# Hybrid MLA/GLA block: finer second norm, eight modulation columns computed later

## Chip, cores and metric

One core of one Trainium2 chip runs the whole kernel. The metric is device time of one execution in microseconds. It is the median of three runs.

## What is computed

One decoder block in float32 for 512 tokens of width 2048. Two token mixers (latent attention and gated linear attention) run side by side, and a SwiGLU feed-forward network follows. Both halves are normed before and after, and modulated by six vectors that are linear in silu(c). The part that the change touches is this:

```python
ada = silu(c) @ w_ada + b_ada                       # 6 x 2048 columns
shift_m, scale_m, gate_m, shift_f, scale_f, gate_f = split(ada, 6)
...
o = concat([o_mla, o_gla]) @ w_out
x = x + gate_m * rms_norm(o, g_post_mix)            # first half of the second norm
h = rms_norm(x, g_pre_ffn) * (1 + scale_f) + shift_f
f = (silu(h @ w_gate) * (h @ w_up)) @ w_down
x = x + gate_f * rms_norm(f, g_post_ffn)
```

## The kernel before

**Products.** Each float32 weight block of 128 x 2048 is loaded by SP into one of four buffers of the pool `wr` and split into a rounded part and a remainder. ACT makes the first (`CAST`, L202 and L910), DVE the second (`TENSOR_TENSOR`, L203 and L911). Both land in eight buffers `wh`. Three matmuls (L214 to L216) make one product.

**Modulation columns.** `ada` (L224) loads 1 MB of `w_ada` into a `wr` buffer (L227), and one DVE operation (L228) multiplies it by the broadcast silu(c) and sums each row: 128 of the 12288 columns. The broadcast itself holds one `wr` buffer until the last of them. The generator `ada_rest` hands out 64 of these steps, one for each `next(more)`: gate_m, scale_f, shift_f, gate_f, in blocks of 16. The filler steps consume them: `fill_qk` four per step, `fill_vr` three, `fill_out` one or two.

**Output projection.** `out_group` (L881) multiplies the GLA half of the mixed rows by a column block n of `w_out`, in two steps q. It adds the attention half that was spilled earlier (L891), sums squares (L892) and multiplies by gate and gain (L893). Column block 0 is done for all four token tiles. Then blocks 1 to 3 are done for tiles 0 and 1 (th = 0), and for tiles 2 and 3 (th = 1).

**Second norm.** `second_norm(t)` takes one token tile: row scale, residual add (L808), squares (L810), second row scale. Then for each n it scales the rows (L817), transposes four 128 x 128 pieces on PE (L820) and modulates them on ACT (L826). The columns land in `h2`. It is a generator, and `advance(k)` takes k steps of it. The norms of tiles 0 and 1 are advanced in the projection of th = 1. Those of tiles 2 and 3 are advanced in the early products.

**Early products and forms.** The feed-forward network uses a seven-product scheme on a 2 x 2 split (token half by feature half). Each of its inputs is a form, a block of `h2` or a sum of blocks, split into two parts by `parts` (ACT `CAST` L837, DVE L838). The differences are DVE `minus` (L842). The first six blocks (`PRO` = 6) compute two of the products early, 12 banks of 48 matmuls, from the forms a11 and a12. These need tiles 0 and 1 alone. Meanwhile `more_forms` makes s1, s3, s2, a22 and s4, which need tiles 2 and 3. The main loop uses these from its first products on. A finished bank is emptied by ACT (L940) or DVE (`vadd`, L928).

**Order.** A scheduler places the instructions on each engine's queue from the order of the program and from pool releases. Each queue runs in order.

Of the kernel before, what the change touches and what calls it, by code (L numbers as in the profile page):

```python
# [14 lines left out]
AF = mybir.ActivationFunctionType  # L15
ALU = mybir.AluOpType
# [4 lines left out]
P = 128  # L21
S = 512
D = 2048
KT = D // P
DFF = 5632
NT = S // P
# [51 lines left out]
def block_kernel(ctx, tc, x, c, pos, w_ada, cols, w_g1, w_kqvr, w_uq, w_uk, w_uv, wg17,  # L78
# [9 lines left out]
    V, A, T = nc.vector, nc.scalar, nc.tensor  # L88
# [22 lines left out]
    def t2(dt=F32, n=512):  # L111
        return sp.tile([P, n], dt, tag="t2k", name=nm("t"))

    def bank(g):
        return pp.tile([P, 512], F32, tag="ps" + g, name=nm("ps"), bufs=4)
# [18 lines left out]
    bias = cp.tile([P, 4], F32, name="bias")  # L134
# [3 lines left out]
    ident = cs[:, K_ID:K_ID + P]  # L138
# [6 lines left out]
    for n in range(4):  # L145
        ps = bank("A")
# [4 lines left out]
    def rsqrt(src, n, w=1):  # L151

        v, y, b = small(w, "rv"), small(w, "ry"), small(w, "rb")
        V.tensor_scalar(v, src, 1.0 / n, EPS, op0=ALU.mult, op1=ALU.add)
        last_act[0] = A.activation(y, v, AF.Sqrt)
        V.reciprocal(y, y)
        V.scalar_tensor_tensor(out=b, in0=v, scalar=-0.5, in1=y, op0=ALU.mult, op1=ALU.mult)
        V.tensor_tensor(out=b, in0=b, in1=y, op=ALU.mult)
        V.scalar_tensor_tensor(out=y, in0=b, scalar=1.5, in1=y, op0=ALU.add, op1=ALU.mult)
        return y  # L160
# [30 lines left out]
    def load_split(src, nkt, ncol):  # L191

        raw = wp.tile([P, 2048], F32, tag="wr", name=nm("wr"))
        dma(out=raw[:, :nkt * ncol], in_=src)
        per = 1024 // ncol if ncol <= 1024 else 1
        parts = []
        for k0 in range(0, nkt, per):
            n = min(per, nkt - k0) * ncol
            r = raw[:, k0 * ncol:k0 * ncol + n]
            hi = wp.tile([P, 1024], F32R, tag="wh", name=nm("hi"), bufs=8)  # L200
            lo = wp.tile([P, 1024], F32R, tag="wh", name=nm("lo"), bufs=8)
            A.copy(out=hi[:, :n], in_=r)  # L202
            V.tensor_tensor(out=lo[:, :n], in0=r, in1=hi[:, :n], op=ALU.subtract)  # L203
            for k in range(min(per, nkt - k0)):
                parts.append((hi[:, k * ncol:(k + 1) * ncol], lo[:, k * ncol:(k + 1) * ncol]))
        return parts
# [27 lines left out]
    scol = cp.tile([P, 32], F32, name="scol")  # L234
    shcol = cp.tile([P, 32], F32, name="shcol")
# [33 lines left out]
    for t in range(NT):  # L269
        for n in range(4):  # L270
            acc, xx = xs[:, 4 * t + n:4 * t + n + 1], xt_[t][n]
            if t == NT - 1:
                V.tensor_tensor_reduce(out=sq[1], in0=xx, in1=xx, scale=1.0, scalar=0.0,
                                       op0=ALU.mult, op1=ALU.add, accum_out=acc)
# [140 lines left out]
    for which, src in ((0, ang), (1, al)):  # L415
        ps = bank("B")
# [39 lines left out]
    def fill_qk():  # L456
        for half in range(2):
            pss = [bank("A") for _ in range(4)]
            for kq in (2, 3):
                w = load_split(w_kqvr[half, kq], 4, 512)  # L460
                for _ in range(4):
                    next(more)
                for k, b in ORDER[kq == 3]:
                    mm3(pss[b], cut(w[k], b * P, P), hT[4 * kq + k], kq + k == 2, kq + k == 6)
                if kq == 3:
                    add_up(pss, qk[4 * half:4 * half + 4])
                    qk[4 * half:4 * half + 4] = spill(qk[4 * half:4 * half + 4], "qk")
                yield
# [327 lines left out]
    x1d = [dp.tile([P, D], F32, name=f"x1d{t}") for t in range(NT)]  # L796
    mixg = [split_new(o) for o in mixg]
    osum = cp.tile([P, 16], F32, name="osum")
    def second_norm(t):
        v = small(1, "v1")  # L800
        V.tensor_reduce(out=v, in_=osum[:, 4 * t:4 * t + 4], axis=AX.X, op=ALU.add)
        v = rsqrt(v, D)
        xs = small(4, "xs")
        xt = wp.tile([P, 2048], F32, tag="wr", name=nm("wr"))
        dma(out=xt, in_=x[t])
        for n in range(4):
            xs_ = xt[:, n * 512:(n + 1) * 512]
            V.scalar_tensor_tensor(out=og[t][n], in0=og[t][n], scalar=v, in1=xs_, op0=ALU.mult, op1=ALU.add)  # L808
            dma2(out=x1d[t][:, n * 512:(n + 1) * 512], in_=og[t][n])
            A.activation(xs_, og[t][n], AF.Square, accum_out=xs[:, n:n + 1])  # L810
        v2 = small(1, "v2")
        V.tensor_reduce(out=v2, in_=xs, axis=AX.X, op=ALU.add)
        v2 = rsqrt(v2, D)
        yield
        for n in range(4):
            y = t2()
            A.activation(y, og[t][n], AF.Copy, scale=v2)  # L817
            ps = bank("B")
            for k in range(4):
                T.transpose(ps[:, k * P:(k + 1) * P], y[:, k * P:(k + 1) * P], ident)  # L820
            for k in range(4):
                kk = 4 * n + k
                if kk % 2 == 0 and t % 2 == 0:
                    h2[t // 2][kk // 2] = t2()
                o = (kk % 2) * 256 + (t % 2) * P
                A.activation(h2[t // 2][kk // 2][:, o:o + P], ps[:, k * P:(k + 1) * P], AF.Identity,  # L826
                             scale=scol[:, 16 + kk:17 + kk], bias=shcol[:, 16 + kk:17 + kk])
            yield

# [3 lines left out]
    def parts(src):  # L835
        hi, lo = t2(F32R), t2(F32R)
        A.copy(out=hi, in_=src)  # L837
        V.tensor_tensor(out=lo, in0=src, in1=hi, op=ALU.subtract)  # L838
        return hi, lo

    def minus(out, a, b):
        V.tensor_tensor(out=out, in0=a, in1=b, op=ALU.subtract)  # L842
# [1 line left out]
    h2 = [[None] * 8, [None] * 8]  # L844
    form = {n: [None] * 4 for n in ("a11", "a12", "a22", "s1", "s2", "s3", "s4")}

    def first_forms():
        for j in range(4):
            form["a11"][j] = parts(h2[0][j])
            yield  # L850
        for j in range(4):
            form["a12"][j] = parts(h2[0][4 + j])
            yield

    def more_forms():
        s2 = [None] * 4
        for j in range(4):
            a11, a21, a22 = h2[0][j], h2[1][j], h2[1][4 + j]
            s1 = t2()
            minus(s1, a21, a22)  # L860
            form["s1"][j] = parts(s1)
            minus(a21, a21, a11)
            form["s3"][j] = parts(a21)
            minus(a11, a11, s1)
            s2[j] = a11
            form["s2"][j] = parts(a11)
            yield
        for j in range(4):
            form["a22"][j] = parts(h2[1][4 + j])
            a12 = h2[0][4 + j]  # L870
            minus(a12, a12, s2[j])
            form["s4"][j] = parts(a12)
            yield

    norms = iter(())

    def advance(n):
        for _ in range(n):
            next(norms, None)

    def out_group(n, toks, steps=0):  # L881
        pss = {t: bank("A") for t in toks}
        for q in range(2):
            w = load_split(w_out[n, 2 + q], 4, 512)
            for k in range(4):
                for t in toks:
                    mm3(pss[t], cut(mixg[4 * q + k], t * P, P), w[k], q + k == 0, q + k == 4)
            advance(steps)
        for t in toks:
            o = og[t][n] = fetch(og[t][n])  # L890
            V.tensor_tensor(out=o, in0=pss[t], in1=o, op=ALU.add)  # L891
            A.activation(pss[t], o, AF.Square, accum_out=osum[:, 4 * t + n:4 * t + n + 1])  # L892
            V.tensor_tensor(out=o, in0=o, in1=ggm[n], op=ALU.mult)  # L893
# [3 lines left out]
    for th in range(2):  # L897
        toks = (2 * th, 2 * th + 1)
        for n in range(1, 4):
            out_group(n, toks, 3)  # L900
        advance(30)
        norms = itertools.chain(*[second_norm(t) for t in toks], (first_forms, more_forms)[th]())


    def wtile():
# [2 lines left out]
    def wparts(src):  # L908
        hi, lo = wtile(), wtile()
        A.copy(out=hi, in_=src)  # L910
        V.tensor_tensor(out=lo, in0=src, in1=hi, op=ALU.subtract)  # L911
        return hi, lo
# [6 lines left out]
    def up_product(ps, w, f, s, first, last):  # L919

        for kk in range(4):
            rh = cut(form[f][2 * s + kk // 2], (kk % 2) * 256, 256)
            for b in range(2):
                mm3(ps[:, b * 256:(b + 1) * 256], cut(w, kk * 256 + b * P, P), rh,
                    first and kk + b == 0, last and kk + b == 4)
# [5 lines left out]
    for j in range(PRO):  # L931
        raws = [raw_of(w_fg[j, s]) for s in range(2)]
        q1, sg = t2(), t2()
        for f, o in (("a11", 0), ("a12", 1024)):
            ps = bank("A")
            for s in range(2):
                up_product(ps, wparts(raws[s][:, o:o + 1024]), f, s, s == 0, s == 1)
                advance(2)
            if f == "a11":
                A.copy(out=q1, in_=ps)  # L940
        vadd(sg, ps, q1)
        A.activation(sg, sg, AF.Silu)
        early.append((q1, sg))
    advance(30)

    gd = []
    gate_f = gate_out(1)
# [230 lines left out]
```

## Time and profile before

| | |
|---|---|
| median of three runs | 2164.9 us (2156.6 to 2166.36) |
| profiled execution, its own time | 2170.64 us |
| its span | 2168.9 us |
| PE busy | 2081.8 us (96%) |
| DVE busy | 1752.8 us (81%) |
| ACT busy | 918.8 us (42%) |

Times on the timeline count from the start of the span. The granted TensorE clock is a share of full speed. A busy PE can still be at half clock, so idle time and clock are read together, stage by stage.

### The profile page before, as it was taken

To read this page: it belongs to the slowest core of one execution; us is meant where nothing else is said; L and a number is where in the kernel's file an instruction comes from. 1 tells how busy PE (TensorE), PEld (TensorE's weight loads), DVE (VectorE), ACT (ScalarE), POOL (GpSimd) and SP (SyncE) were. 2 spreads that over 40 slices of the span, in tenths; PEclk is the share of its full clock that TensorE was granted. 3 is DMA by queue.
4 is the path that set the end of the run, shared out by engine and by line. 5 is a ranking of instruction groups with operands and counts; after the bars stand their busy time and mean duration, and the time that the engine had idled before them with its cause. 6 is when DMAs were issued, how large, how long until landed. Compare 5 with 4: busy or idle time off the path is not lost.

```text
span 2168.9 us, 31978 instructions
## 1 busy us (share of the span) xinstructions
PE 2081.8 (96%) x12714; PEld 1841.0 (85%) x12714; DVE 1752.8 (81%) x2236; ACT 918.8 (42%) x1277; POOL 206.0 (9%) x387
## 2 busy tenths in 40 slices
PE   7999999999899996999999999999999999999998
PEld 5888767776688875999999999999999988888876
DVE  6888987667466676789998898888888877988998
ACT  5433223233332487444344444444444454333342
POOL 0000000001111010010011011011001031221000
PEclk9999999999899997999999999999999999999999
DMA  8886787567365564354544344343344665564534
GB/s 335 303 323 235 278 304 270 221 229 269 119 244 212 185 244 172 120 197 165 205 160 166 127 165 156 127 175 147 127 175 150 274 261 205 213 237 155 206 116 156
DMA packets 85818, 440.56 MB, mean 203 GB/s; under 512 B 12297, under 2 KB 12409, under 8 KB 48034
## 3 DMA queue, kind: packets, MB, share of 16 engines
q1 hardware_dynamic: 55440, 340.16, 42.8%
q0 software_dynamic: 30224, 98.33, 12.0%
q8 instruction: 100, 1.64, 0.3%
q14 instruction: 52, 0.42, 0.1%
q10 hardware_dynamic: 2, 0.01, 0.0%
HBM read 379.19 MB, written 59.26 MB: 202 GB/s over the span
## 4 chain that ended last, share of the span: by engine, by line
PE 70%; issue 15%; DVE 8%; DMA 5%; ACT 1%; POOL 1%; SPq 0%; DVEq 0%; ACTq 0%; POOLq 0%
PE ps L214 22%; PE ps L215 22%; PE ps L216 22%; DMA wr<-w_ada 3%; DVE wr L228 2%; DVE t L928 1%; DMA wr<-w_kqvr 1%; DVE wh L911 1%; DVE lo L203 1%; PE ps L584 1%; PE ps L611 1%; DVE wr L928 1%; PE ps L583 1%; DMA t<-x 0%; DMA wr<-w_uq 0%
## 5 line engine op out<-in xcount | busy, mean ns | idle before, releaser
L214 PE MATMUL ps<-t,wh 128*128 128x256 f32 x2464 | 703.0, 285 | 20.9 <-DVE t L928 8.2
L910 ACT CAST wh<-wr 128x1024 fp32r<-128x1024 f32 x448 | 464.7, 1051 | 592.8 <-PE ps L215 335.1
L216 PE MATMUL ps<-t,wh 128*128 128x256 f32 x2464 | 701.1, 285 | 2.9 <-DVE wh L911 2.7
L215 PE MATMUL ps<-t,wh 128*128 128x256 f32 x2464 | 701.5, 285 | 0.0
L911 DVE TENSOR_TENSOR wh<-wr,wh 128x1024 fp32r<-128x1024 f32 x448 | 540.7, 1220 | 141.1 <-ACT wh L910 138.2
L214 PEld LDWEIGHTS ps<-t,wh 128*128 128x128 f32 x2464 | 477.5, 194 | 23.4 <-issue 8.4
L216 PEld LDWEIGHTS ps<-t,wh 128*128 128x128 f32 x2464 | 477.0, 194 | 3.5 <-DVE wh L911 3.5
L215 PEld LDWEIGHTS ps<-t,wh 128*128 128x128 f32 x2464 | 477.5, 194 | 0.0
L228 DVE CUSTOM_DVE_ANT_0 wr<-wr,cB 128x2048 f32<-128x2048 f32 x96 | 219.3, 2286 | 47.7 <-DMA wr<-w_ada 47.4
L202 ACT CAST hi<-wr 128x1024 fp32r<-128x1024 f32 (+3 forms) x122 | 122.6, 1009 | 241.8 <-PE ps L215 145.2
L215 PE MATMUL ps<-wh,t 128*128 128x512 f32 x560 | 218.1, 389 | 3.0 <-DVE wh L911 3.0
L216 PE MATMUL ps<-wh,t 128*128 128x512 f32 x560 | 217.7, 389 | 0.0
L214 PE MATMUL ps<-wh,t 128*128 128x512 f32 x560 | 217.2, 389 | 0.0
L928 DVE TENSOR_TENSOR wr<-wr,wr 128x1024 f32<-128x1024 f32 (+1 forms) x128 | 198.7, 1554 | 16.2 <-DMA wr<-w_fd 13.9
L203 DVE TENSOR_TENSOR lo<-wr,hi 128x1024 fp32r<-128x1024 f32 (+3 forms) x122 | 141.9, 1168 | 55.9 <-ACT hi L202 53.9
L214 PE MATMUL ps<-t,hi 128*128 128x512 f32 x432 | 169.5, 400 | 5.2 <-DVE t L313 2.4
L215 PE MATMUL ps<-t,hi 128*128 128x512 f32 x432 | 171.3, 397 | 2.5 <-DVE t L306 2.4
L216 PE MATMUL ps<-t,lo 128*128 128x512 f32 x432 | 169.6, 394 | 0.0
L214 PE MATMUL ps<-hi,t 128*128 128x512 f32 x400 | 161.6, 404 | 1.2 <-DVE t L209 0.9
L928 DVE TENSOR_TENSOR t<-ps,t 128x512 f32<-128x512 f32 x222 | 149.6, 683 | 9.4 <-issue 7.9
L215 PE MATMUL ps<-lo,t 128*128 128x512 f32 x400 | 156.8, 392 | 0.0
L216 PE MATMUL ps<-hi,t 128*128 128x512 f32 x400 | 156.2, 393 | 0.0
(229 smaller groups left out, 2427.9 us busy)
## 6 DMA issues: line engine op xcount, KB each, us to landing
wr<-w_ada SPq DMA_DIRECT2D x96, 1024.0 KB, 5.6
wr<-w_fg SPq DMA_DIRECT2D x56, 1024.0 KB, 4.9
wr<-w_fu SPq DMA_DIRECT2D x44, 1024.0 KB, 7.1
wr<-w_fd SPq DMA_DIRECT2D x40, 1024.0 KB, 5.9
gd<-t POOLq DMA_DIRECT2D x148, 256.0 KB, 2.7
t<-gd POOLq DMA_DIRECT2D x112, 256.0 KB, 4.6
wr<-w_kqvr SPq DMA_DIRECT2D x24, 1024.0 KB, 5.0
wr<-w_out SPq DMA_DIRECT2D x22, 1024.0 KB, 5.8
```

The lines of the kernel that those rows point to most:

```text
L202: A.copy(out=hi[:, :n], in_=r)
L203: V.tensor_tensor(out=lo[:, :n], in0=r, in1=hi[:, :n], op=ALU.subtract)
L214: T.matmul(ps, lhsT=a, rhs=c_, start=start, stop=False)
L215: T.matmul(ps, lhsT=a, rhs=d_, start=False, stop=False)
L216: T.matmul(ps, lhsT=b, rhs=c_, start=False, stop=stop)
L228: V.tensor_tensor_reduce(out=raw, in0=raw, in1=cB, scale=1.0, scalar=0.0, op0=ALU.mult, op1=ALU.add, accum_out=adac[:, j:j + 1])
L583: T.matmul(sc[:, :W], lhsT=qn[hh][:, qs], rhs=kn[hh][:, :W], start=True, stop=False)
L584: T.matmul(sc[:, :W], lhsT=qr[rows, qs], rhs=krope[rows, :W], start=False, stop=True)
L611: T.matmul(po[:, qs], lhsT=vh[j][:, (h % 4) * P:(h % 4 + 1) * P], rhs=pT[:, j * P:(j + 1) * P], start=(j == 0), stop=(j == i))
L910: A.copy(out=hi, in_=src)
L911: V.tensor_tensor(out=lo, in0=src, in1=hi, op=ALU.subtract)
L928: V.tensor_tensor(out=out, in0=a, in1=b, op=ALU.add)
```

## The change

`fill_qk` takes two modulation steps instead of four, in four steps of the program: eight fewer there. The later fillers take the same numbers as before, and `out_group` now takes one after each load of `w_out`. The 64 steps are used up within th = 0.

The second norm takes a pair of tiles. Both residuals come first. The rows of column block i + 1 are scaled while block i is turned (transposed and modulated). After each block of both tiles the forms that it completes are made, one per step. For tiles 2 and 3 the blocks go in the order 0, 2, 1, 3. The fourth of each four modulations goes to DVE as a `tensor_scalar`. The 30 forced steps between the halves are gone, and the chain of norms goes on. In the early products two steps are taken per product for the first two blocks and one after that. A loop takes more steps where a form is missing.

```diff
             for kq in (2, 3):
                 w = load_split(w_kqvr[half, kq], 4, 512)
-                for _ in range(4):
+                for _ in range(2):
                     next(more)
...
-    def second_norm(t):
+    def residual(t):
...
-        v2 = rsqrt(v2, D)
+        return rsqrt(v2, D)
+
+    def scaled(t, n, v2):
+        ys[t][n] = y = t2()
+        A.activation(y, og[t][n], AF.Copy, scale=v2)
+
+    def turned(t, n):
+
+        ps = bank("B")
+        for k in range(4):
+            T.transpose(ps[:, k * P:(k + 1) * P], ys[t][n][:, k * P:(k + 1) * P], ident)
...
+            if k == 3:
+                V.tensor_scalar(dst, src, sc, sh, op0=ALU.mult, op1=ALU.add)
+            else:
+                A.activation(dst, src, AF.Identity, scale=sc, bias=sh)
+
+    def second_norm(toks, order, then):
+
+        a, b = toks
+        va = residual(a)
         yield
...
+        vb = residual(b)
+        yield
+        for i, n in enumerate(order):
+            if i == 0:
+                scaled(a, n, va)
+                scaled(b, n, vb)
+                yield
+            if i < 3:
+                scaled(a, order[i + 1], va)
+            turned(a, n)
             yield
+            if i < 3:
+                scaled(b, order[i + 1], vb)
+            turned(b, n)
+            yield
+            for _ in then(i):
+                yield
...
+    def more_forms(i):
+        if i % 2 == 0:
+            return
+        for j in (i - 1, i):
...
             form["s1"][j] = parts(s1)
+            yield
             minus(a21, a21, a11)
             form["s3"][j] = parts(a21)
+            yield
...
             w = load_split(w_out[n, 2 + q], 4, 512)
+            next(more)
...
-        advance(30)
-        norms = itertools.chain(*[second_norm(t) for t in toks], (first_forms, more_forms)[th]())
+        norms = itertools.chain(norms, second_norm(toks, ORDERS[th], (first_forms, more_forms)[th]))
+    while form["a11"][1] is None:
+        advance(1)
...
-                up_product(ps, wparts(raws[s][:, o:o + 1024]), f, s, s == 0, s == 1)
-                advance(2)
+                w = wparts(raws[s][:, o:o + 1024])
+                while form[f][2 * s + 1] is None:
+                    advance(1)
+                up_product(ps, w, f, s, s == 0, s == 1)
+                advance(2 if j < 2 else 1)
```

On the SP queue, the loads of the output projection stood like this before (`wr` is the weight pool, L194 a weight load, L805 the load of x for a residual):

```order
L194 DMA wr_5508<-w_out 128x2048
L194 DMA wr_5542<-w_out 128x2048
L194 DMA wr_5588<-w_out 128x2048
L805 DMA wr_5634<-x 128x2048
L194 DMA wr_5685<-w_out 128x2048
L805 DMA wr_5757<-x 128x2048
L194 DMA wr_5794<-w_out 128x2048
```

and stand like this now (L808 is the load of x):

```order
L194 DMA wr_5502<-w_out 128x2048
L227 DMA wr_5512<-w_ada 128x2048
L194 DMA wr_5539<-w_out 128x2048
L227 DMA wr_5549<-w_ada 128x2048
L194 DMA wr_5588<-w_out 128x2048
L808 DMA wr_5634<-x 128x2048
L808 DMA wr_5671<-x 128x2048
L194 DMA wr_5700<-w_out 128x2048
```

The modulation loads alternate with the weight loads, and the second load of x moved ahead of the second weight load of th = 1.

On the DVE queue, column blocks 2 and 3 of th = 0 stood like this before (L203 is a remainder of `w_out`, L891 and L893 empty the banks of a block):

```order
L203 TENSOR_TENSOR lo_5511<-wr_5508,hi_5510 128x1024
L203 TENSOR_TENSOR lo_5515<-wr_5508,hi_5514 128x1024
L203 TENSOR_TENSOR lo_5545<-wr_5542,hi_5544 128x1024
L891 TENSOR_TENSOR t_5496<-ps_5426,t_5496 128x512
L891 TENSOR_TENSOR t_5501<-ps_5427,t_5501 128x512
L203 TENSOR_TENSOR lo_5549<-wr_5542,hi_5548 128x1024
```

and stand like this now (L923 empties the banks, L228 is the modulation step):

```order
L203 TENSOR_TENSOR lo_5505<-wr_5502,hi_5504 128x1024
L228 ISA wr_5512,adac<-wr_5512,cB 128x2048
L203 TENSOR_TENSOR lo_5509<-wr_5502,hi_5508 128x1024
L923 TENSOR_TENSOR t_5490<-ps_5414,t_5490 128x512
L923 TENSOR_TENSOR t_5495<-ps_5415,t_5495 128x512
L203 TENSOR_TENSOR lo_5542<-wr_5539,hi_5541 128x1024
```

One modulation step now stands among the four remainders of each column block, ahead of the two that empty the banks.

On the ACT queue, the norms of tiles 2 and 3 in the early products stood like this before (L817 scales rows, L826 modulates, L810 sums squares, L940 empties a bank):

```order
L817 ACTIVATE t_6100<-t_5336,ry_6092 128x512
L910 CAST wh_6579<-wr_6528 128x1024
L826 ACTIVATE t_6107<-ps_6102,shcol,scol 128x128 x2
L826 ACTIVATE t_6110<-ps_6102,shcol,scol 128x128 x2
L817 ACTIVATE t_6141<-t_5782,ry_6092 128x512
L810 ACTIVATE wr_6222,xs_6221<-t_5341 128x512
L810 ACTIVATE wr_6222,xs_6221<-t_5787 128x512
L826 ACTIVATE t_6148<-ps_6143,shcol,scol 128x128 x2
```

and stand like this now (L813 sums squares, L943 splits a weight, L820 scales rows, L837 modulates, L976 empties a bank):

```order
L820 ACTIVATE t_6165<-t_5318,ry_6092 128x512
L943 CAST wh_6480<-wr_6443 128x1024
L813 ACTIVATE wr_6140,xs_6139<-t_5323 128x512
L813 ACTIVATE wr_6140,xs_6139<-t_5767 128x512
L813 ACTIVATE wr_6140,xs_6139<-t_5896 128x512
L813 ACTIVATE wr_6140,xs_6139<-t_6019 128x512
L943 CAST wh_6515<-wr_6441 128x1024
L155 ACTIVATE ry_6157<-rv_6156 128x1
L943 CAST wh_6556<-wr_6443 128x1024
L820 ACTIVATE t_6167<-t_5323,ry_6157 128x512
L976 COPY t_6028<-ps_6030 128x512
L820 ACTIVATE t_6199<-t_5891,ry_6092 128x512
```

The squares of tile 3 now come before the second tile's first scaled rows, and so before most of the modulations. On PE the first transpose of tile 2 comes 18 matmuls sooner, after 174 matmuls of the early products instead of 192, and the first of tile 3 is the second group of transposes instead of the fifth.

## Rows read from the trace of the kernel before

**Rows 1.** Windows: window, length, busy us (count) by engine, PEclk, DMA share, GB/s

```profile
215.00:345.00 130.00, 125.43 (x534) 95.59 (x534) 111.28 (x175) 34.10 (x59) 7.15 (x13) 0.99 0.79 289
700.00:760.00 60.00, 60.00 (x266) 49.70 (x265) 43.51 (x62) 27.91 (x46) 4.11 (x9) 1.00 0.55 201
760.00:793.58 33.58, 28.88 (x137) 22.27 (x136) 20.89 (x40) 31.91 (x73) 5.66 (x11) 1.00 0.78 286
793.58:900.92 107.34, 83.65 (x606) 81.34 (x607) 75.06 (x114) 68.54 (x126) 4.35 (x8) 0.84 0.44 157
880.00:900.00 20.00, 20.00 (x169) 20.00 (x169) 14.18 (x13) 8.84 (x10) 0.00 (x0) 1.00 0.53 198
```

**Rows 2.** Waits of PE, 760 to 900: line, releaser, us in total, times, longest

```profile
PE ps L820 <- ACT t L817: 9.2, 5, 3.2
PE ps L214 <- DVE t L928: 8.2, 1, 8.2
PE ps L214 <- ACT t L940: 7.6, 2, 5.5
```

**Rows 3.** Timeline of PE, early products: start, us, instruction [idle before <-releaser]

```profile
793.59 0.39 PE L214 MATMUL ps<-t,wh 128*128 128x256 f32 x1 [2.06 <-ACT ps L892]
...
844.63 0.42 PE L214 MATMUL ps<-t,wh 128*128 128x256 f32 x1
844.84 0.42 PE L215 MATMUL ps<-t,wh 128*128 128x256 f32 x1
...
847.83 0.33 PE L214 MATMUL ps<-t,wh 128*128 128x256 f32 x1
...
854.24 0.58 PE L214 MATMUL ps<-t,wh 128*128 128x256 f32 x1 [5.49 <-ACT t L940]
...
870.20 0.55 PE L214 MATMUL ps<-t,wh 128*128 128x256 f32 x1 [8.22 <-DVE t L928]
...
874.81 0.41 PE L214 MATMUL ps<-t,wh 128*128 128x256 f32 x1
```

**Rows 4.** Timeline of DVE, 840 to 873

```profile
840.84 2.14 DVE L842 TENSOR_TENSOR t<-t,t 128x512 f32<-128x512 f32 x3 [9.24 <-ACT t L826]
...
869.37 0.68 DVE L928 TENSOR_TENSOR t<-ps,t 128x512 f32<-128x512 f32 x1
```

**Rows 5.** DVE by line and form, 215 to 345: busy, mean ns, idle before

```profile
L228 DVE CUSTOM_DVE_ANT_0 wr<-wr,cB 128x2048 f32<-128x2048 f32 x24 | 54.8, 2283 | 4.9 <-DMA wr<-w_ada 4.6
...
L585 DVE TENSOR_TENSOR ps<-ps,cs 128x128 f32<-128x128 f32 x8 | 2.2, 291 | 3.4 <-PE ps L584 3.4
```

**Rows 6.** Waits of PE, 215 to 345

```profile
PE ps L604 <- ACT t L591: 3.0, 2, 2.1
```

**Rows 7.** Chain of waits, 215 to 345, one load: start, us

```profile
293.36 8.75 DMA wr<-w_kqvr
```

**Rows 8.** Timeline of DVE, one column block of the output projection, th = 0

```profile
735.73 1.22 DVE L203 TENSOR_TENSOR lo<-wr,hi 128x1024 fp32r<-128x1024 f32 x1 [1.49 <-ACT hi L202]
738.45 1.23 DVE L203 TENSOR_TENSOR lo<-wr,hi 128x1024 fp32r<-128x1024 f32 x1 [1.50 <-ACT hi L202]
739.63 1.37 DVE L891 TENSOR_TENSOR t<-ps,t 128x512 f32<-128x512 f32 x2
...
750.51 1.37 DVE L891 TENSOR_TENSOR t<-ps,t 128x512 f32<-128x512 f32 x2
```

**Rows 9.** Page, DMA issues: KB each, median us from issue to landing

```profile
wr<-w_ada SPq DMA_DIRECT2D x96, 1024.0 KB, 5.6
```

**Rows 10.** ACT by line and form, 790 to 880

```profile
L826 ACT ACTIVATE t<-ps,shcol,scol 128x128 f32<-128x128 f32 x32 | 11.9, 461 | 2.2 <-PE ps L820 2.2
L817 ACT ACTIVATE t<-t,ry 128x512 f32<-128x512 f32 x8 | 5.6, 730 | 1.8 <-DVE ry L159 1.8
L810 ACT ACTIVATE wr<-t 128x512 f32<-128x512 f32 x8 | 5.0, 633 | 2.8 <-DVE t L808 2.8
```

More of the change, by code (lines that the diff above doesn't have):

```diff
@@ L798, in block_kernel @@
     osum = cp.tile([P, 16], F32, name="osum")
-    def second_norm(t):
+    ys = [[None] * 4 for _ in range(NT)]
+    def residual(t):
         v = small(1, "v1")
@@ L812, in second_norm @@
         V.tensor_reduce(out=v2, in_=xs, axis=AX.X, op=ALU.add)
-        v2 = rsqrt(v2, D)
-        yield
[L815 to L827, printed above, removed]
-            yield
+        return rsqrt(v2, D)
[6 more added lines that the diff above has]
+            T.transpose(ps[:, k * P:(k + 1) * P], ys[t][n][:, k * P:(k + 1) * P], ident)
+        for k in range(4):
+            kk = 4 * n + k
+            if kk % 2 == 0 and t % 2 == 0:
+                h2[t // 2][kk // 2] = t2()
+            o = (kk % 2) * 256 + (t % 2) * P
+            dst, src = h2[t // 2][kk // 2][:, o:o + P], ps[:, k * P:(k + 1) * P]
+            sc, sh = scol[:, 16 + kk:17 + kk], shcol[:, 16 + kk:17 + kk]
+            if k == 3:
[5 more added lines that the diff above has]
+        va = residual(a)
+        yield
+        vb = residual(b)
[8 more added lines that the diff above has]
+            turned(a, n)
+            yield
+            if i < 3:
[4 more added lines that the diff above has]
+                yield
     def parts(src):
@@ L845, in block_kernel, with first_forms @@
     form = {n: [None] * 4 for n in ("a11", "a12", "a22", "s1", "s2", "s3", "s4")}
-    def first_forms():
-        for j in range(4):
-            form["a11"][j] = parts(h2[0][j])
+    def first_forms(i):
+        for j in (2 * i, 2 * i + 1):
+            form[("a11", "a12")[j // 4]][j % 4] = parts(h2[0][j])
             yield
[L851 to L858, printed above, removed]
+    def more_forms(i):
+        if i % 2 == 0:
+            return
+        for j in (i - 1, i):
+            a11, a21, a22, a12 = h2[0][j], h2[1][j], h2[1][4 + j], h2[0][4 + j]
             s1 = t2()
@@ L861, in more_forms @@
             form["s1"][j] = parts(s1)
+            yield
             minus(a21, a21, a11)
             form["s3"][j] = parts(a21)
+            yield
             minus(a11, a11, s1)
-            s2[j] = a11
             form["s2"][j] = parts(a11)
             yield
[L868 to L871, printed above, removed]
+            form["a22"][j] = parts(a22)
+            yield
+            minus(a12, a12, a11)
             form["s4"][j] = parts(a12)
@@ L875, in block_kernel @@
     norms = iter(())
+    ORDERS = (range(4), (0, 2, 1, 3))
     def advance(n):
@@ L943, in block_kernel @@
         early.append((q1, sg))
-    advance(30)
+    advance(60)
     gd = []
```

## The prediction, made before the changed kernel ran

> **What bounds the kernel now.** I read the windows first, since a mean over the whole program hides stages. From 700 to 760 us PE is busy for the whole 60.00 us at full clock [rows 1], so no change to other engines can speed that stage up, only slow it. Two places are different. From 760 to 793.58, the output projection of th = 1, PE is busy 28.88 of 33.58 us: 4.7 us lost. From 793.58 to 900.92, the early products, PE is busy 83.65 of 107.34 us, and its mean granted clock is 0.84 [rows 1]. The stage ends where the main loop's first product starts.
>
> The reader can work out what the early products need. They are 12 banks of 48 matmuls, 576 in all. From 880 to 900, without a wait and at full clock, 169 start in 20.00 us [rows 1], one every 0.1183 us. That makes 68.2 us. Eight groups of four transposes take about 0.5 us each in the stream, 4.1. The sum is 72.3 us, so 107.3 - 72.3 = 35 us are lost there.
>
> Where the 35 us go is in the list of PE's waits and its timeline. PE waits 9.2 us for the scaled rows of the norm, 8.2 us for DVE to empty a bank and 7.6 us for ACT to empty a bank [rows 2]. The two long waits, 5.49 at 854.24 and 8.22 at 870.20 [rows 3], are late consequences. DVE stood idle for 9.24 us up to 840.84, since it had no modulated columns. Then it did the differences and remainders of all forms in one piece, and a bank's `vadd` reached its turn only at 869.37 [rows 4]. After each long wait the rows run slow: 844.63 to 844.84 is 0.21 us apart, which is the level of 1.2 GHz in place of 2.4 [rows 3]. That explains the clock of 0.84.
>
> The third place is the filler stage, 215 to 345: PE busy 125.43 of 130 us at a mean clock of 0.99, while DVE is busy 111.28 us and the DMA share is 0.79 [rows 1].
>
> **The change, part by part.**
>
> *Eight modulation steps leave the fillers.* They take 8 x 2.28 us of DVE [rows 5] = 18.3 us, and 8 loads of 1 MB, about 29 us of DMA at the 289 GB/s of that stage [rows 1]. PE loses at most 130 - 125.43 = 4.6 us of idle time, plus about 1.3 us (0.01 of the clock over 130 us), 5.9 in all. Of the idle time 3.0 us is a wait of the attention for its exponentials on ACT [rows 6], which this part does not touch directly. A load that landed late, 8.75 us [rows 7], helped to make it so. The gain lies between -2 (the attention's waits grow as its operands meet in another order, 2.1 being the longest now) and 5.9. I take **-3 us**, half the cap.
>
> *The eight steps enter the output projection.* In the new DVE order five of them stand in 700 to 750, the other three earlier. In that stage DVE is busy 43.51 of 60 us [rows 1]. A column block takes 750.51 - 739.63 = 10.88 us [rows 8], of which DVE works 0.725 x 10.88 = 7.9. One step of 2.28 us per block makes 10.2, so it fits. But DVE must also wait for the step's load, and behind that wait stand the remainder of the next weight and the emptying of the banks. DVE meets a remainder each 2.7 us (735.73, 738.45), and 1.5 us of that is waiting for ACT [rows 8]. A modulation load takes 5.6 us in the median [rows 9]. In the order a load is issued when a remainder frees a buffer, and its step comes one remainder later, so DVE can wait 5.6 - 2.7 = 2.9 us at each. Weight parts are made about two pieces ahead of their use, so most of this delay is absorbed. Bounds: 0, and 5 x 2.9 = 14.5 us if none is. I take **+1**, nearest to the row of 60.00 busy in 60, which says that waits of this size do not reach PE today.
>
> What the row shows of DVE's order is the wait of 9.24 us: nothing else ran on DVE in it [rows 4]. The Trainium skill, page "TensorE: Matmul & The Clock Gate", section "Architectural detail: the array is 16x 32x32, not 1x 128x128", says that ScalarE and VectorE queues are strictly first in, first out; the trace agrees, with that 9.24 us. By that rule taken alone, with no work made ahead, the term would be +14.5 us in place of +1, and the total about -4.
>
> *The queue of loads for th = 1.* Both loads of x now stand ahead of the second weight load of th = 1 on SP, and the second x needs the buffer of the last modulation step, about 748. So that weight lands some 3 us later than it is wanted. Following the new order with the old durations I get PE waits of 2.9, 0.8, 2.7 and 1.3 us, 7.7 in all, against 4.7 lost there now [rows 1]. The difference is 3.0; some 0.6 of transposes fall into the waits. I take **+2.4**: the early products start at 793.6 + 2.4 = 796.0. Bounds 0 and +6, one whole load.
>
> *The finer norm.* I followed the orders of ACT, DVE and PE with old durations: scaled rows 0.73, squares 0.63 + 0.2, modulation 0.46 [rows 10], and the nearest row for a modulation on DVE, an operation of 128 x 128 from PSUM with 0.29 [rows 5]. Sixteen such operations cost DVE 4.7 us and spare ACT 16 x 0.46 = 7.4; both lie beside the products, where DVE had 9.24 us idle, and I count no gain of their own. The chain then is this. The first transposes of tile 2 wait 1.6 us. Those of tile 3 wait longest, 5.8 us, since ACT does the four squares, a row scale and two weight casts ahead of its scaled rows. After that the turned blocks come as fast as ACT modulates them, and DVE starts on the forms after two blocks rather than after four; the later waits are 0.3, 0.7, 1.1 and 0.5. The sum is 10.0 us in place of 107.34 - 83.65 = 23.7 [rows 1]. The clock: after the wait of 5.8 us I expect half clock for about 5 us, as from 870.20 to 874.81 [rows 3], which costs some 2.5; two short dips like the one from 844.63 to 847.83 [rows 3], 1.6 each, 3.2; transposes at half clock 1.0. So the stage takes 72.3 + 10.0 + 2.5 + 3.2 + 1.0 = 89.0 us, and the main loop starts at 796.0 + 89.0 = 885.0 in place of 900.9: **-15.9**, which includes the +2.4. Bounds: -25 (half of the waits and no dip) and -6 (a wait of 8.22 us for a bank stays [rows 3]).
>
> *Everything after* keeps its order on PE from the main loop on, so nothing is counted there.
>
> **Sum.** -3 + 1 - 15.9 = -17.9 us. The profiled execution took 2170.64, so 2152.7 by its own time. It is 5.7 us above the median of the runs, 2164.9; from the median the sum gives **2147 us**.
>
> **Rivals.**
>
> *Slower: modulation loads hold up DVE in the output projection.* One mechanism: in five places of 700 to 750 DVE waits for a load that was issued late, and the remainder behind it comes too late for PE. Each such place costs PE the excess over the work made ahead, and 1.6 us of half clock. If a step comes as soon as its load is issued, or the load lands late, as the one of 8.75 us did [rows 7], DVE waits some 5.6 us; five places make 5 x (5.6 + 1.6) = 36, less the 18.9 gained elsewhere: +17, 2182. With the order as it stands and loads at the median it does not happen. It decides at a wait of 4.3 us on PE per place: 5 x (4.3 + 1.6) = 29.5, which is 18.9 + 10.6. For it: three `wr` buffers in place of four in that stage, and queues in order. Against it: the DMA share is only 0.55 there [rows 1]. Chance 0.12.
>
> *No change: the burst only moves.* The forms are still 20 casts and 20 remainders and 16 differences. If ACT and DVE cannot spread them, a bank waits for its emptying behind them, as at 870.20, and the main loop starts some 5 us earlier than now, less 2.4 for the late start: 2.6 + 3 - 1 = about -5, 2160. For it: the two residuals are now serial on ACT ahead of tile 3. Against: DVE had 32 of 107 us free [rows 1]. Chance 0.21.
>
> *Full gain.* The clock never falls and the banks never wait: 35 - 2.4 + 3 - 1 = -34.6, 2130. For it: all the missing work is a matter of order. Against: tile 3's squares stand in one piece ahead of its first scaled rows. Chance 0.10.
>
> *The forecast* has the rest, 0.57.
>
> **How the numbers follow.** A measurement of this kernel can tell about 0.5%, 10.8 us, from no change. Faster by more: nearly all of the forecast (0.54), the full gain (0.10) and a little of the second rival (0.02), 0.66. Slower by more: most of the first rival, 0.10. The rest is 0.24. The range 2130 to 2170 leaves out the slower rival and half of the full gain, some 0.17. The forecast's own bounds are 2134 to 2162: the norm's term and the fillers' at their ends.
>
> **What would show it.** Early products from about 796 to 885, with the largest wait of PE some 6 us on the scaled rows of tile 3 (L820 now), and no wait of 5 us or more for a bank. Granted clock of the stage about 0.92 in place of 0.84. From 700 to 750 PE busy throughout, with L228 waiting for `w_ada` on DVE by some 3 us a time. Fillers from 215 a few us shorter. The prediction is wrong if PE shows waits on L203 in the output projection, if a bank still waits 5 us or more, or if the main loop starts after 893.

## The result, and the profile after

The changed kernel takes 2151.41 us (median of four runs, 2149.52 to 2154.24). Before it is 2163.14 (2156.6 to 2166.36). The ratio is 0.995, 95% interval [0.993, 0.9971]: 11.7 us less, where 17.9 were forecast. The two profiled executions are 2168.9 and 2150.1 us long, 18.8 apart. The difference between 11.7 and 18.8 has to be explained too.

Here are the windows of the changed kernel that answer to [rows 1]: window, length, busy us (count) of PE, weight loads, DVE, ACT and POOL, granted clock, DMA share, GB/s. The last two rows divide at the first early product, 798.09, and the last one ends next to the main loop's first product.

```profile
215.00:345.00 130.00, 129.74 (x568) 99.26 (x567) 106.31 (x176) 37.39 (x66) 7.64 (x14) 1.00 0.68 248
700.00:760.00 60.00, 55.37 (x235) 44.79 (x234) 47.20 (x66) 25.39 (x47) 2.18 (x4) 0.97 0.72 269
760.00:798.09 38.09, 32.38 (x145) 25.65 (x144) 28.12 (x50) 30.67 (x61) 5.37 (x10) 0.91 0.67 259
798.09:881.89 83.80, 76.68 (x614) 75.13 (x612) 69.29 (x115) 63.60 (x119) 4.36 (x8) 0.96 0.55 201
```

The last row is the gain: 83.80 us in place of 107.34, with PE idle 7.1 us in place of 23.7 and a clock of 0.96 in place of 0.84. The second row is a loss: PE was busy for all of 60 us, and now it is for 55.37.

The waits of PE from 700 to 900 us (line, releaser, us in total, times, longest) show both, and answer to [rows 2]:

```profile
PE ps L826 <- ACT t L820: 9.9, 3, 5.2
PE ps L214 <- ACT ps L924: 4.0, 2, 3.0
PE ps L214 <- ACT hi L202: 1.1, 1, 1.1
PE ps L214 <- ACT t L976: 1.1, 1, 1.1
```

The waits of 5.49 and 8.22 us for a bank [rows 3] are gone; L976, which answers to L940, has 1.1. A new one stands in the second row: 3.0 us for L924, the squares in the output projection. Its place in PE's timeline, and the rest of PE's larger waits (start, us, instruction, idle before):

```profile
716.28 0.79 PE L214 MATMUL ps<-hi,t 128*128 128x512 f32 x1 [3.01 <-ACT ps L924]
716.88 0.63 PE L215 MATMUL ps<-lo,t 128*128 128x512 f32 x1
717.30 0.63 PE L216 MATMUL ps<-hi,t 128*128 128x512 f32 x1
...
769.19 0.66 PE L826 MATMUL ps<-cs,t 128*128 128x128 f32 x4 [1.76 <-ACT t L820]
...
781.92 1.12 PE L826 MATMUL ps<-cs,t 128*128 128x128 f32 x4 [2.98 <-ACT t L820]
...
827.35 1.12 PE L826 MATMUL ps<-cs,t 128*128 128x128 f32 x4 [5.20 <-ACT t L820]
...
844.67 0.39 PE L214 MATMUL ps<-t,wh 128*128 128x256 f32 x1 [1.06 <-ACT t L976]
...
881.34 0.28 PE L214 MATMUL ps<-t,wh 128*128 128x256 f32 x1
```

After 716.28 the matmuls start 0.42 us apart (716.88, 717.30): half clock again, a granted clock of 0.50 from 716.3 to 719.5. The same place on DVE's timeline says why:

```profile
702.78 2.29 DVE L228 CUSTOM_DVE_ANT_0 wr<-wr,cB 128x2048 f32<-128x2048 f32 x1 [2.27 <-DMA wr<-w_ada]
...
712.57 2.29 DVE L228 CUSTOM_DVE_ANT_0 wr<-wr,cB 128x2048 f32<-128x2048 f32 x1 [2.62 <-DMA wr<-w_ada]
...
714.79 1.88 DVE L923 TENSOR_TENSOR t<-ps,t 128x512 f32<-128x512 f32 x3
```

At 712.57 DVE had waited 2.62 us for a modulation load, worked 2.29 us, and only then emptied the banks of column block 0. PE needed one of them. Block 0 is done for four token tiles and so holds all four banks of its pool (`bank("A")`), while the later blocks hold two. The step at 702.78 waited 2.27 us with remainders behind it, and PE shows no wait there. The other three of the five steps, from 725 on, did not wait for their loads at all.

### The profile page after: what moved, and what is told of

Read it like the earlier page. It is cut to its first block, busy times and chain, and to the rows that moved or that the text cites. A ratio compares the mean times of both kernels' runs of the same rounds, so it can differ in the third digit from the quotient of the medians.

```text
span 2150.1 us, 31995 instructions
## 1 busy us (share of the span) xinstructions
PE 2078.5 (97%) x12714; PEld 1836.8 (85%) x12714; DVE 1758.2 (82%) x2252; ACT 912.3 (42%) x1261; POOL 206.2 (10%) x387
## 4 chain that ended last, share of the span: by engine, by line
PE 72%; issue 16%; DVE 6%; DMA 3%; ACT 1%; POOL 1%; SPq 0%; DVEq 0%; POOLq 0%; ACTq 0%
PE ps L216 22%; PE ps L215 22%; PE ps L214 22%; DMA wr<-w_ada 2%; DVE wh L944 1%; DVE t L961 1%; DVE wr L961 1%; PE ps L584 1%; DVE wr L228 1%; PE ps L583 1%; PE ps L611 1%; DMA t<-x 1%; DMA wr<-w_fu 0%; DVE t L874 0%; PE ps L604 0%
## 5 line engine op out<-in xcount | busy, mean ns | idle before, releaser
L943 ACT CAST wh<-wr 128x1024 fp32r<-128x1024 f32 x448 | 463.9, 1050 | 580.9 <-PE ps L215 317.8
L228 DVE CUSTOM_DVE_ANT_0 wr<-wr,cB 128x2048 f32<-128x2048 f32 x96 | 219.3, 2286 | 53.7 <-DMA wr<-w_ada 53.6
L203 DVE TENSOR_TENSOR lo<-wr,hi 128x1024 fp32r<-128x1024 f32 (+3 forms) x122 | 141.8, 1168 | 49.7 <-ACT hi L202 49.1
```

Source lines behind the costliest of these rows:

```text
L228: V.tensor_tensor_reduce(out=raw, in0=raw, in1=cB, scale=1.0, scalar=0.0, op0=ALU.mult, op1=ALU.add, accum_out=adac[:, j:j + 1])
```

## The experiments

All stages are compared by three marks: G, the first matmul of the output projection (the row with 0.9 us of waiting for the remainder of L209); E, the first early product; and M, the first product of the main loop. M is counted: it is the 577th matmul on a part of a feed-forward weight (`wh`), and in every trace the 576th ends a bank. It starts at 901.29 before and at 881.34 in the changed kernel. From M to the end the kernels are alike only within some us: 1267.6 before, 1266.9 in e1, 1268.8 in the changed kernel, 1268.5 in e4, and between 1265.2 (e12) and 1270.0 (e6, e7) in the others. What sets these differences was not tried, so a shorter E to M is not all gain. The expectations of e6 to e10 name 84.9 us for the early products of the norm-only kernel. That figure is the span less 1268.1 less E, as if the rest took the same time in all kernels; counted, it is 84.5. The ratios come from the timed runs, with their 95% intervals; the marks from one profile each.

| kernel | ratio to before | G | G to E | E to M |
|---|---|---|---|---|
| before | | 696.4 | 97.2 | 107.7 |
| before, again (e1) | 1.0007 [0.9992, 1.0022] | 691.2 | 97.8 | 105.6 |
| modulation steps only (e2) | 1.0034 [1.0019, 1.005] | 688.4 | 110.2 | 105.4 |
| norm only (e3) | 0.991 [0.9887, 0.9934] | 694.8 | 100.8 | 84.5 |
| the changed kernel | 0.995 [0.993, 0.9971] | 691.2 | 106.9 | 83.2 |
| the changed kernel, again (e4) | 0.9939 [0.9914, 0.9963] | 692.9 | 108.2 | 83.9 |
| one step put back (e5) | 0.9901 [0.9885, 0.9918] | 694.2 | 101.3 | 83.8 |
| norm only, all modulations on ACT (e6) | 0.9923 [0.9905, 0.994] | 688.8 | 100.7 | 85.3 |
| norm only, plain block order (e7) | 0.9915 [0.9896, 0.9934] | 689.3 | 99.8 | 83.0 |
| norm only, rows not ahead (e8) | 0.9929 [0.9908, 0.995] | 691.2 | 99.5 | 87.9 |
| norm only, forms in lumps (e9) | 0.9935 [0.9922, 0.9949] | 690.4 | 99.7 | 93.3 |
| norm only, tile by tile (e10) | 0.9909 [0.9883, 0.9935] | 690.5 | 99.2 | 89.4 |
| four steps moved (e11) | 0.9896 [0.9878, 0.9914] | 700.0 | 98.7 | 84.1 |
| four steps moved, adds first (e12) | 0.987 [0.9845, 0.9896] | 689.9 | 95.8 | 86.2 |

**e1, before again.** No edit.

> The kernel before, unchanged, as a null measurement and for a second profile. Theory 1 (the profiled execution of before, 2170.64 us, was a long one of this kernel, and its extra 6 to 8 us sit in stages with half clock): ratio 1.00 within 0.3%, the new profile takes 2156 to 2166 us, and the early products take less than 107.3 us or the stretch from 500 to 640 us fewer slow matmuls. Theory 2 (the profiled stages are always like that and the profile itself costs some us): the new profile again takes about 2170 us with the early products at 107 us.

Ratio 1.0007. The new profile is 2161.6 us long, 7.3 shorter than the first, with the same instructions. G comes 5.2 us earlier, and the early products take 2.1 us less. So theory 1: the first profile of before was a long execution. PE's longest wait from 215 to 345 us is 1.3 us in the new profile, where [rows 6] has one of 2.1.

**e2, the modulation steps alone.**

```diff
-                for _ in range(4):
+                for _ in range(2):
                     next(more)
...
             w = load_split(w_out[n, 2 + q], 4, 512)
+            next(more)
```

> Only the eight modulation steps are moved, the second norm is as before. Theory 1 (the fillers gain 5 us, the output projection loses as much or more, since DVE waits for the loads there): within 3 us of before, early products start about 3 us later than 793.6 to 3 us earlier. Rival (the output projection absorbs them, its waits come from the norm's loads of x): 4 to 6 us faster than before.

It is slower than before, by 0.34% or 7 us, more than theory 1 allowed, and the rival is out. The stretch from G to E grew from 97.5 us (mean of the two profiles of before) to 110.2. PE's row shows the same wait as in the changed kernel (below). It is not all of the 12.7 us: in th = 1 PE waits 8.4 us for scaled rows, where before it waits 2.2, and the granted clock from G to E is 0.94 in place of 1.00. What lengthened the waits of th = 1 here was not tried.

```profile
713.76 0.55 PE L214 MATMUL ps<-hi,t 128*128 128x512 f32 x1 [3.30 <-ACT ps L893]
```

**e3, the norm alone.** The changed kernel with four steps in the fillers and none in the output projection.

```diff
-                for _ in range(2):
+                for _ in range(4):
                     next(more)
...
             w = load_split(w_out[n, 2 + q], 4, 512)
-            next(more)
```

> Only the second norm is changed, the fillers take four modulation steps per step as before and the output projection none. Theory 1 (the norm carries nearly the whole gain): 10 to 16 us faster than before in the timed runs, early products 82 to 86 us long, no wait of 3 us on a square's bank near 716 us. Rival (the two parts help each other, the shorter fillers are half of the gain): 4 to 7 us faster.

0.991, 2146.1 us: faster in its median than the changed kernel beside it (e4, 2151.6), although the intervals overlap. E to M is 84.5 us, and PE has no wait near 716 us. The norm carries the whole gain. That the moved steps take some of it back is shown by G to E and by e2, not by these two times.

**e4, the changed kernel again.** No edit.

> The changed kernel, unchanged, timed beside the other three: 10 to 14 us faster than before; its profile takes 2149 to 2154 us with the early products at 83 to 85 us.

As expected: 11 us faster than before, early products 83.9 us. The wait on L924 is 4.0 us here.

**e5, one modulation step put back.** The step at block 2, step 0, is the one that stands on DVE ahead of the banks of block 0.

```diff
-                for _ in range(2):
+                for _ in range(3 if half + kq == 2 else 2):
                     next(more)
...
             w = load_split(w_out[n, 2 + q], 4, 512)
-            next(more)
+            if (n, q) != (2, 0):
+                next(more)
```

> The changed kernel, but the one modulation step whose load DVE waits for ahead of the four banks of column block 0 is taken in the fillers again (three in the first filler step, none at block 2, step 0). Theory 1 (the output projection's loss is that one place: DVE stands 2.3 to 3.6 us for a load with the emptying of the banks behind it): the PE wait of 3.0 to 4.0 us near 716 us is gone, the stretch from the start of the output projection to the first early product takes 102 to 104 us in place of 107 to 108, and the kernel is 3 to 6 us faster than the changed kernel, near 2147. Rival (each of the steps costs its share, as DVE and the loads are slower all along): at most 1 us faster than the changed kernel, another wait takes its place.

G to E is 101.3 in place of 106.9 and 108.2, and the median is 2141.4, against 2151.4 and 2151.6 for the changed kernel. The interval [0.9885, 0.9918] stays below that of the first measurement, [0.993, 0.9971], and touches the lower end of e4's. On DVE the emptying of the banks waits for PE again, and not for a load:

```profile
714.27 2.05 DVE L924 TENSOR_TENSOR t<-ps,t 128x512 f32<-128x512 f32 x3 [1.32 <-PE ps L216]
```

So without this step G to E is 5.6 to 6.9 us shorter. Of this 3.0 to 4.0 are the wait, and about 1.6 the half clock behind it (half of the 3.2 us from 716.3 to 719.5). The rest is a stretch of half clock in th = 1, behind a wait of 2.98 us that all three have: 0.50 from 781.2 to 787.7 in the changed kernel, and here only from 781.6 to 784.8. It is not shown to belong to the step, since e3, with none moved, has 0.50 from 779.8 to 786.4. So the place cost about 4.6 to 5.6 us. The other moved steps cost little: PE waits 1.1 us for a late weight near 755, which e3 does not show. The median fell by 10 us, more than the marks account for; the profile is of the longest of the four executions (2150.05 us; the others take 2140.1 to 2142.4).

**e6, all modulations on ACT.** From here to e10 the diffs leave out the lines of e3, which all five share.

```diff
-            if k == 3:
-                V.tensor_scalar(dst, src, sc, sh, op0=ALU.mult, op1=ALU.add)
-            else:
-                A.activation(dst, src, AF.Identity, scale=sc, bias=sh)
+            A.activation(dst, src, AF.Identity, scale=sc, bias=sh)
```

> The norm alone changed, with all four modulations of a block on ACT. Theory 1 (the order of the forms carries the gain, the 16 operations lie beside the products): early products within 2 us of the 84.9 us of the norm-only kernel, time within 3 us of its 2146. Rival (ACT is what the norm waits for, its 16 operations of 0.35 to 0.46 us are on the path): early products 4 to 7 us longer.

Early products 85.3 us, 0.8 more, and the time (2146.4) is not told apart from that of e3. Theory 1 holds.

**e7, the plain order of blocks.**

```diff
-    ORDERS = (range(4), (0, 2, 1, 3))
+    ORDERS = (range(4), range(4))
...
-        if i % 2 == 0:
+        if i < 2:
             return
-        for j in (i - 1, i):
+        for j in (2 * i - 4, 2 * i - 3):
```

> The norm alone changed, but the blocks of tiles 2 and 3 in the order 0, 1, 2, 3, so that no form of the second half can be made before the third block. Theory 1 (the gain comes from DVE starting on the forms early, after two blocks): early products 5 to 12 us longer than 84.9, with a wait for a bank of 3 us or more. Rival (the gain comes from one form per step, which lets the emptying of the banks in between): within 2 us of 84.9.

83.0 us, 1.5 less than in e3: theory 1 falls here. That forms can be made after two blocks rather than three is worth nothing that shows. One wait for a bank of 1.7 us came back and no more.

**e8, rows not scaled ahead.**

```diff
-            if i == 0:
-                scaled(a, n, va)
-                scaled(b, n, vb)
-                yield
-            if i < 3:
-                scaled(a, order[i + 1], va)
+            scaled(a, n, va)
             turned(a, n)
             yield
-            if i < 3:
-                scaled(b, order[i + 1], vb)
+            scaled(b, n, vb)
             turned(b, n)
```

> The norm alone changed, but rows are scaled just before they are turned and not one block ahead. Theory 1 (rows scaled ahead keep PE from waiting on ACT): PE waits for scaled rows 3 to 6 us more than the 11.0 us of the norm-only kernel between 640 and 910 us, early products 3 to 5 us longer. Rival (scaling ahead only moves work of ACT ahead of the second tile's first rows): within 2 us, with a shorter longest wait than 5.9 us.

Early products 87.9 us, 3.4 longer, as theory 1 had it, but by another way: the waits for scaled rows are 8.8 us in place of 11.0, and 3.8 us of waiting for a bank (`vadd`) came back. The longest wait is 6.4. Two of the ten groups of transposes between E and M are of tiles 0 and 1 and stand ahead of E in the other kernels, so that 1 us of the 3.4, by the prediction's 0.5 a group, only moved.

**e9, forms in lumps.** No `yield` between s1, s3 and s2, nor between a22 and s4.

```diff
             form["s1"][j] = parts(s1)
-            yield
             minus(a21, a21, a11)
             form["s3"][j] = parts(a21)
-            yield
...
             form["a22"][j] = parts(a22)
-            yield
             minus(a12, a12, a11)
```

> The norm alone changed, but the forms of the second half come in lumps again: s1, s3 and s2 of a block in one step, a22 and s4 in one step. Theory 1 (one form per step is what lets DVE and ACT empty banks in between): waits for banks of 3 us or more come back, early products 88 to 95 us in place of 84.9. Rival (the two tiles taken together, with forms after half of the blocks, carry the gain): within 2 us of 84.9.

93.3 us, and the wait for a bank is back, as theory 1 said. PE's waits from 790 to 882 us:

```profile
PE ps L214 <- ACT t L972: 8.7, 2, 6.7
PE ps L826 <- ACT t L820: 5.8, 2, 5.2
```

**e10, tile by tile.** The old order of the norm, with the new forms behind it.

```diff
-        a, b = toks
...
+        for t in toks:
+            v2 = residual(t)
+            yield
+            for n in order:
+                scaled(t, n, v2)
+                turned(t, n)
+                yield
+        for i in range(4):
+            for _ in then(i):
+                yield
```

> The norm alone changed, but each tile is normed as a whole, tile 2 and then tile 3, with no rows scaled ahead; the forms come afterwards, one per step. Theory 1 (one form per step carries the gain): early products 85 to 92 us, no wait for a bank over 3 us. Rival (the order of the tiles carries it): DVE again stands idle for 5 us or more ahead of the forms and the early products take 97 us or more.

89.4 us, within theory 1's 85 to 92; the rival's 97 is out. DVE's longest wait there is 2.7 us, not 9.24 [rows 4]. Fine forms without the pairing of tiles bring 106.7 (mean of before) to 89.4, and the pairing without fine forms (e9) brings it to 93.3. Both together give 84.5. The two remedies largely take away the same loss. Both runs keep the rest of the new norm: the modulation on DVE, which e6 prices at 0.8 us, and the new stepping (no 30 forced steps, two steps per product and then one). No run takes the stepping back alone, so part of either saving may be its own.

**e11, four steps moved.** The changed kernel with three steps per filler step. The four moved ones end within block 1 of th = 0 in the program.

```diff
-                for _ in range(2):
+                for _ in range(3):
                     next(more)
```

> The changed kernel with three modulation steps per filler step, so that only four move to the output projection and none stands among its blocks for tiles 0 and 1 beyond the first. Theory 1 (moved steps are free where DVE does not wait for their load ahead of a bank): start of the output projection 691 to 693 us, 100 to 102 us from there to the early products, 1 to 4 us faster than the norm-only kernel's 2146 and 6 to 9 us faster than the changed kernel. Rival (the fillers gain nothing from fewer steps): within 1 us of the norm-only kernel.

2141.5 us. G to E is 98.7 us, 2.1 less than in e3 and 8.2 to 9.5 less than in the changed kernel. Only one of the four runs after G, at 712.55. DVE waits 3.24 us for its load, and PE does not wait at all. G itself, 700.0, missed the expected 691 to 693. The profiled execution is the longest of the six (2153.6 us; the others take 2140.5 to 2142.9), but 2.4 us of the delay have a cause in its rows. A step stands ahead of the operations that PE needs next, and its load is late:

```profile
690.75 2.29 DVE L228 CUSTOM_DVE_ANT_0 wr<-wr,cB 128x2048 f32<-128x2048 f32 x1 [4.58 <-DMA wr<-w_ada]
...
695.13 1.13 PE L184 MATMUL ps<-t,ones 128*128 128x512 f32 x2 [2.40 <-DVE t L178]
```

With the same fillers e12 has a wait of 1.24 us at this place, and G is 689.9. So a step that waits for its load can cost in the fillers too.

Against e3 the medians differ by 4.6 us, but the ratios' intervals overlap, so a gain over leaving all steps in the fillers is likely and not shown.

**e12, adds first.** On top of e11 the residual adds of both tiles come ahead of either tile's squares. The diff leaves out that `residual` now ends before the squares, which are `squared`.

```diff
...
-        va = residual(a)
+        xa = residual(a)
         yield
-        vb = residual(b)
+        xb = residual(b)
+        va = squared(a, *xa)
+        yield
+        vb = squared(b, *xb)
         yield
```

> The half-moved kernel (three modulation steps per filler step, four in the output projection), and in the norm both residual adds come ahead of the squares of either tile, so that the two row-scale chains run side by side. Theory 1 (the longest wait left, 5.9 us for tile 3's scaled rows, is the second chain waiting behind the first): the two waits for scaled rows at the start of tiles 2 and 3 together take 3 to 5 us in place of 6.6, early products 81 to 83.5 us, 1 to 4 us faster than the half-moved kernel's 2141.5. Rival (the wait only moves from tile 3 to tile 2, since ACT does the squares of both ahead of any rows): the two waits together stay at 6 to 7 us and the time within 1 us of 2141.5.

Theory 1 held in its waits for scaled rows and in the time: the median is 2136.2 us, 5.3 less than e11, though the two intervals overlap a little. It did not hold for the early products, which take 86.2 us, 2.1 more than in e11, where 81 to 83.5 were expected. PE's waits from 785 to 869 us have no 5.9 any more:

```profile
PE ps L214 <- ACT wh L950: 3.5, 4, 1.3
PE ps L830 <- ACT t L824: 2.9, 2, 2.1
PE ps L216 <- DVE wh L951: 2.0, 2, 1.1
```

The two waits for scaled rows take 2.9 us in place of e11's 6.5. More came back as waits for weights (3.5 and 2.0, against 0.9 in e11). The gain stands elsewhere: G to E fell to 95.8, below before, and M to the end to 1265.2, against 1269.1 in e11. In th = 1 the wait for scaled rows is no shorter (3.05, e11 2.98); a wait of 1.0 us for a bank is gone. What made the rest of either gain is open. At 0.987 [0.9845, 0.9896] the kernel is faster than both kernels of this case.

## Why the prediction came out as it did

It was right in direction and in its range (2147 with 2130 to 2170; measured 2151.4). The gain of 11.7 us is two thirds of the 17.9 forecast. Term by term:

- **The finer norm, forecast at 89.0 us of early products, starting at 796.0.** They took 83.2 us from 798.1. The walk through the new orders gave the waits closely: 1.6 and 5.8 forecast for the first rows of tiles 2 and 3, 0 and 5.20 measured; 1.1 forecast for the longest later wait, 1.06 measured (for a bank). The two extra clock dips (3.2 us) did not come: from 840 to 860 the clock is 1.00. Between the means of two profiles each, 106.7 before and 83.6 now, the term is -23.1 where -18.3 (89.0 - 107.3) was forecast. The second rival ("the burst only moves") is out.
- **Why it works** was half right. The prediction had the late start of DVE, 9.24 us idle [rows 4], as the root. e7 shows that an earlier start through the block order is worth nothing. e9 and e10 show that breaking the lump of differences and remainders, or pairing the tiles, does most of it, with the new stepping, which no run took back alone. I had followed the lump, `vadd` at 869.37 [rows 4], only as a consequence. One reading was wrong as well: the slow rows from 844.63 [rows 3] stand behind waits of 0.66, 0.17 and 0.76 us, not behind one of the two long waits.
- **The modulation on DVE** takes 0.41 us rather than the 0.29 of [rows 5]. The nearest row had another operation; L835 is in the rows below. e6 shows 0.8 us in the stage and nothing in the total.
- **The eight steps in the output projection, forecast at +1.** This is the step that failed. Measured, 106.9 and 108.2 us from G to E against 100.8 without them (e3): +6.1 to +7.4. The forecast had DVE wait up to 2.9 us at each of the five places, and let the work made ahead absorb it. In the changed kernel DVE waited at two, 2.27 and 2.62 us (2.18 and 3.62 in e4). The first has remainders behind it and was absorbed. The second has the banks of block 0 behind it, and was not: with all four banks held, PE waits until one is emptied. e5 takes this place away and G to E falls to 101.3; the place itself cost about 4.6 to 5.6 us. The prediction's own sign, PE busy throughout from 700 to 750, did not come (55.37 of the 60 us from 700 to 760), and one of its signs of being wrong did, a wait of PE for L203 in the output projection, though of 0.52 us only. With nothing absorbed, as the strict queue of VectorE alone would have it (the Trainium skill, page "TensorE: Matmul & The Clock Gate", section "Architectural detail: the array is 16x 32x32, not 1x 128x128"), the term was +14.5 by the prediction's sum; the runs lie between the two. So the first rival's mechanism was at work, in one place of five. There its price on PE was 3.0 to 4.0 us of wait, short of the 4.3 per place at which the rival was to decide, and it reversed nothing since the norm's gain was three times as large. Alone (e2) the move makes the kernel slower.
- **The loads of th = 1, forecast at +2.4 for the start.** Without any moved step G to E grew from 97.5 to 100.8 (e3), +3.3; the waits there are for scaled rows, 1.5 and 3.0 us, and for a bank, 1.4, not for the weight. They are 5.9 in all, against 4.6 and 5.3 in the two profiles of before, and the granted clock from G to E is 0.97 in place of 1.00. In the changed kernel the weight is late too, 1.1 us at 757 in place of the 2.9 walked out.
- **The fillers, forecast at -3.** Not seen in G. G is 688.8 to 696.4 us in eight profiles with four steps per filler step (mean 691.6), and 688.4 to 692.9 in three with two (mean 690.8). A gain under 1 us lies within what one execution differs from the next. The timed runs leave it open: e5 and e11, with seven and four steps moved, have medians 4.7 and 4.6 us below e3's with none, but the intervals overlap.
- **The base.** The sum was made against an execution that was long by its own accident. G at 696.4 and early products of 107.7 are both high (e1: 691.2 and 105.6). 18.8 us between two profiles are 11.7 us between medians. Taking the difference off the median, as the text did, kept the forecast in place, but terms were sized on that long execution.

By the measured terms: -23.1 (early products), +3.3 (th = 1), +6.7 (moved steps), -0.8 (fillers) and +1.4 from M to the end, where nothing was counted (mean 1267.3 before, 1268.7 now), make -12.5, near the -11.7 of the timed runs. That 2151.4 lies so near 2147 is partly luck: the norm gave 4.8 us more than forecast, and the moved steps 5.7 and the fillers 2.2 less.

The row of the modulation on DVE in the changed kernel, 790 to 880 us by line and form (busy, mean ns, idle before):

```profile
L835 DVE TENSOR_SCALAR t<-ps,scol,shcol 128x128 f32<-128x128 f32 x11 | 4.5, 407 | 7.4 <-ACT t L837 6.2 <-PE ps L216 1.2
```

## What to carry to other kernels

When an operation that waits for a transfer is moved onto an in-order queue, look at what stands directly behind it. A producer that works ahead can absorb the wait, but the emptying of an accumulator bank does not where no other bank is free, so put such steps behind the emptying or leave them out at that one place. Lumps of side work (forms, splits) hurt through the bank whose emptying stands behind them: hand them out one per product, and check each half of such a remedy alone, since two of them may be curing the same loss. Check also that what follows a stage takes the same time in all kernels before a stage is called shorter. Take a second profile of the kernel before, before terms are sized on one execution.

## What was not expected of the hardware

The same instructions up to G took 688.8 to 696.4 us in eight profiles with four steps per filler step. With three it was 700.0 and 689.9. One profile has 42 us busy of 45 from 300 to 345 at a clock of 0.96, another 45.00 of 45 at 1.00 (before, and e1):

```profile
300.00:345.00 45.00, 42.00 (x182) 31.37 (x181) 33.39 (x55) 13.28 (x26) 2.17 (x4) 0.96 0.75 270
```

```profile
300.00:345.00 45.00, 45.00 (x203) 33.88 (x204) 37.01 (x59) 14.98 (x28) 2.70 (x5) 1.00 0.80 286
```

What decides between the two was not tried. In the changed kernel the waits of 3.01 us at 716 and 2.98 at 782 were followed by half clock as the one of 5.20 was (0.42 us between matmuls of 512 columns after 716; a granted clock of 0.51 from 781.9 to 788). After those of 1.1 us at 757, 1.76 at 769 and 1.06 at 844 the clock stayed at 1.00 in the next 6 us. The length of one wait does not decide it alone: in the kernel before, the three waits of 0.66, 0.17 and 0.76 us between 841.5 and 844.4 were followed by 0.50 from 844.6 to 847.9.
